# Modulation chunks of a two-layer block chain, summed over partitions by transposes and reductions in place of products with a pick matrix

## The chip, the cores and the metric

The kernel runs on one core of a Trainium2 chip. The metric is the device time of one launch in microseconds; the median of three runs of the kernel before is 2060.99 us (2060.79 to 2061.44). TensorE (PE) multiplies into PSUM, VectorE (DVE) and ScalarE (ACT) work beside it, and the loads go through the queue of SyncE (SP).

## What is computed

Two blocks of two layers each, on 256 tokens of width 1024. In the first block every layer has a modulation: a vector c (and in layer 0 a second one, c_ctx, for the context) goes through silu and a 1024 x 6144 matrix, and the six pieces of the result shift, scale and gate what the mixer and the feed-forward network (FFN) do.

```python
for i in range(DEPTH):
    mod = jax.nn.silu(c) @ w_ada[i] + b_ada[i]
    mod_c = jax.nn.silu(c_ctx) @ w_ada[i] + b_ada[i]
    sh1, sc1, g1, sh2, sc2, g2 = jnp.split(mod[:, None, :], 6, axis=-1)
    h = _modulate(_rms_norm(x, norm_mix[i]), sh1, sc1)
    ...
    x = x + g1 * y
    x = x + g2 * _swiglu(_modulate(_rms_norm(x, norm_ffn[i]), sh2, sc2), ffn_w_in[i], ffn_w_out[i])
```

Layer 0 mixes with a gated convolution (three 1024 x 1024 projections, then one out), layer 1 with attention. The second block (FFNs, two other mixers) has no modulation and is not touched.

## The kernel before

**Products and weights.** Each large product is made of three: high x high, low x high and high x low, where a float32 is split into a rounded high part and the rest (lines L243, L244, L245). Weights come in units of 512 KB through `WeightStream`: five raw buffers are loaded in a fixed order by SP, each unit is cast to whi on ACT (L106) and subtracted to wlo on DVE (L107) in two halves, with four buffers of whi and wlo. A raw buffer is loaded again when what reads it is done, so a unit that is used late holds back all loads behind it.

**Modulation chunks.** The modulation vector has 12 chunks of 512 columns in each layer. Some are made at the start by other functions. The other 20 are made by `ada_slow`, one (layer, j) at a time, of two vectors (12 chunks: layer 0, and layer 1 up to j = 3) or one (8 chunks). DVE multiplies the raw units with the values of the vector that lie in the partitions: per vector a TENSOR_SCALAR (L476) and seven multiply-adds (L478) of 128x512 into ada_acc. What is left is a sum over the 128 partitions. For it ada_acc is split into ada_hi (ACT, L251) and ada_lo (DVE, L252). A stage later PE multiplies each with `pick`, a matrix of ones and zeros in which one column picks the row of the vector (L489, L490; 2x512 in one PSUM bank), and ACT copies the two rows out (L492). Another stage later `ada_columns` turns the rows into columns by four small transposes (L441), and DVE adds the bias (L444) into mod.

**When they run.** `ada_slow` is a generator. The table ADA_AT starts a chunk at each of these points: the four groups of the convolution's input, groups 0 and 2 of its output for the first 256 tokens (chunks (0,8) and (0,9)), the ten groups of the FFN's hidden part and four of its output part. `ada_at` moves every pending generator on by one stage at each point; `ada_flush` ends them before the modulation of the FFN and of layer 1 needs them. The accumulators have two buffers for each vector (pool `ada`), so a chunk needs the buffer of the chunk two before it.

**What sets the order.** Each engine works through its instructions in a fixed order, which the framework's list scheduler makes from the program's order, the dependencies and its own estimates. So a change of one stage moves instructions of all engines around it. In conv_out (the convolution's output) the products of 256 columns go first for X (256 tokens, v = 0, four groups of 48 matmuls), then for C, the context; after a group DVE adds it to X (L546) and to a sum of squares (L558), and the row statistics (L361, Newton steps L265 to L269, L374, L376) precede the modulation of the FFN's input.

## Time and profile before

| what | us |
|---|---|
| median of three runs (2060.79 to 2061.44) | 2060.99 |
| the profiled execution | 2061.66 |
| its span in the trace | 2059.9 |
| PE busy | 2022.4 |
| DVE busy | 1522.6 |
| ACT busy | 1062.4 |

The profiled execution is 1.8 us longer than its span, the part of a launch that lies outside the trace. Times of places are us from the start of the span. A matmul's recorded length includes the time in the pipeline, so what one costs in a row is the distance to the next one's start.

### The profile page before, as it was taken

How to read it: one execution, taken by the hardware profiler on the slowest of the kernel's cores; microseconds unless marked ns; L12 is line 12 of the kernel's file. 1: busy time of each engine (PE TensorE's matmuls, PEld its weight loads, DVE VectorE, ACT ScalarE, POOL GpSimd, SP SyncE). 2: the span in 40 equal slices, each digit the busy share in tenths (PEclk: the TensorE clock that was granted, in tenths of full speed). 3: DMA queues.
4: the chain of work that ended last, by engine and by line, in shares of the span. 5: the costliest groups of instructions: out<-in, count | busy, mean ns of one | idle time of the engine just before them, and what ended most of it. 6: DMA issues, size and time to landing. Idle time of an engine off the chain costs nothing. (4 is left out here: it accounts for less than half of the span.)

```text
span 2059.9 us, 32409 instructions
## 1 busy us (share of the span) xinstructions
PE 2022.4 (98%) x12430; PEld 1776.4 (86%) x12430; DVE 1522.6 (74%) x2796; ACT 1062.4 (52%) x1763; POOL 4.1 (0%) x24
## 2 busy tenths in 40 slices
PE   7999999999999999999999999999999999999999
PEld 3888887888899999888888889998888888989888
DVE  6979998766377778766677667787767776887774
ACT  4534533323355566555455546555545554675552
POOL 0000000000000000000000000000000000000000
PEclk9999999999999999999999999999999999999999
DMA  7746566656254324466566564556656656425554
GB/s 249 230 144 195 174 206 197 219 189 200 89 165 148 98 88 137 138 186 188 180 190 186 178 189 137 151 171 189 189 176 192 185 183 190 138 83 166 186 180 133
DMA packets 327434, 350.93 MB, mean 170 GB/s; under 512 B 12592, under 2 KB 301488, under 8 KB 327280
## 3 DMA queue, kind: packets, MB, share of 16 engines
q1 hardware_dynamic: 327280, 348.88, 54.8%
q8 instruction: 97, 1.59, 0.3%
q14 instruction: 57, 0.47, 0.1%
HBM read 347.78 MB, written 1.05 MB: 169 GB/s over the span
## 5 line engine op out<-in xcount | busy, mean ns | idle before, releaser
L106 ACT CAST whi<-wraw 128x512 fp32r<-128x512 f32 (+1 forms) x803 | 617.0, 791 | 713.0 <-issue 245.4
L107 DVE TENSOR_TENSOR wlo<-wraw,whi 128x512 fp32r<-128x512 f32 (+1 forms) x803 | 709.5, 900 | 343.5 <-ACT whi L106 340.5
L306 PE MATMUL pg<-x,whi 128*128 128x512 f32 x1408 | 387.9, 397 | 0.5 <-DVE x L255 0.3
L306 PEld LDWEIGHTS pg<-x,whi 128*128 128x128 f32 x1408 | 241.0, 188 | 33.9 <-DVE x L255 2.8
L306 PE MATMUL po<-s,whi 128*128 128x512 f32 x880 | 243.0, 394 | 0.0
L308 PEld LDWEIGHTS pg<-x,wlo 128*128 128x128 f32 x1408 | 215.1, 188 | 31.8
L308 PE MATMUL pg<-x,wlo 128*128 128x256 f32 x1408 | 223.3, 280 | 0.0
L243 PE MATMUL pm<-xh,whi 128*128 128x512 f32 (+1 forms) x576 | 217.2, 381 | 2.8 <-ACT xh L251 2.8
L244 PE MATMUL pm<-xl,whi 128*128 128x512 f32 (+1 forms) x576 | 218.4, 380 | 0.0
L245 PE MATMUL pm<-xh,wlo 128*128 128x512 f32 (+1 forms) x576 | 217.9, 379 | 0.0
L478 DVE SCALAR_TENSOR_TENSOR ada_acc<-wraw,sil,ada_acc 128x512 f32<-128x512 f32 x224 | 159.6, 751 | 24.0 <-DMA wraw<-in_w_ada 22.6
L306 PEld LDWEIGHTS po<-s,whi 128*128 128x128 f32 x880 | 148.7, 189 | 18.0
L308 PEld LDWEIGHTS po<-s,wlo 128*128 128x128 f32 x880 | 137.5, 188 | 20.5
L308 PE MATMUL po<-s,wlo 128*128 128x256 f32 x880 | 142.5, 280 | 0.0
L243 PEld LDWEIGHTS pm<-xh,whi 128*128 128x128 f32 x576 | 109.1, 190 | 25.7 <-ACT xh L251 4.1
L244 PEld LDWEIGHTS pm<-xl,whi 128*128 128x128 f32 x576 | 109.5, 190 | 20.6 <-DVE xl L252 0.2
L245 PEld LDWEIGHTS pm<-xh,wlo 128*128 128x128 f32 x576 | 109.2, 190 | 20.5
L245 PE MATMUL pm<-sh,wlo 128*128 128x256 f32 (+1 forms) x384 | 119.3, 311 | 0.7 <-DVE wlo L107 0.7
L243 PE MATMUL pm<-sh,whi 128*128 128x256 f32 (+1 forms) x384 | 119.2, 311 | 0.0
L244 PE MATMUL pm<-sl,whi 128*128 128x256 f32 (+1 forms) x384 | 118.9, 310 | 0.0
L245 PE MATMUL pm<-whi,xl 128*128 128x256 f32 x352 | 99.7, 283 | 0.0
L306 PE MATMUL pg<-xh,whi 128*128 128x512 f32 x352 | 96.1, 394 | 0.0
(435 smaller groups left out, 3467.4 us busy)
## 6 DMA issues: line engine op xcount, KB each, us to landing
wraw<-in_ffn_w_in SPq DMA_DIRECT2D x264, 512.0 KB, 3.6
wraw<-in_ffn_w_out SPq DMA_DIRECT2D x128, 512.0 KB, 3.5
wraw<-in_w_ada SPq DMA_DIRECT2D x96, 512.0 KB, 4.5
wraw<-in_a_w_in SPq DMA_DIRECT2D x28, 512.0 KB, 3.8
wraw<-in_conv_w_in SPq DMA_DIRECT2D x24, 512.0 KB, 4.7
wraw<-in_attn_w_qkv SPq DMA_DIRECT2D x24, 512.0 KB, 4.0
wraw<-in_conv_w_out SPq DMA_DIRECT2D x16, 512.0 KB, 4.3
wraw<-in_ffn_w_out SPq DMA_DIRECT2D x28, 256.0 KB, 2.7
```

The lines of the kernel that those rows point to most:

```text
L106: self.nc.scalar.copy(hi[:, cs], raw[:, cs])
L107: self.nc.vector.tensor_tensor(lo[:, cs], raw[:, cs], hi[:, cs].bitcast(F32), ALU.subtract)
L243: mm(ps, ah, bh, start=first, stop=False)
L244: mm(ps, ah, bl, start=False, stop=False)
L245: mm(ps, al, bh, start=False, stop=last)
L306: self.nc.tensor.matmul(pss[c], hi[:, kk, cs], x2[:, done + kk], start=done + kk == 0, stop=False)
L308: self.nc.tensor.matmul(pss[c][:, 0, :], lo[:, kk, cs], x2[:, done + kk, 0, :], start=False, stop=done + kk == nblocks - 1)
L478: nc.vector.scalar_tensor_tensor(accs[v], w[:, kk, :], c, accs[v], ALU.mult, ALU.add)
```

## The change

Per chunk and vector the split into ada_hi and ada_lo is gone. At the chunk's next point PE transposes the four 128x128 blocks of ada_acc in fp32 into a PSUM bank, and DVE adds up each row of 128 by a TENSOR_REDUCE into a small tile ada_sum; one more addition puts the bias on, into mod. The products with pick, the row copy on ACT and the small transposes of these chunks are gone, and so is pick. The chunk is done one point earlier, while ada_acc is read by PE at that point and no longer only by ACT and DVE right after the last multiply-add.

```diff
--- before.py
+++ after.py
@@ -59,7 +59,7 @@
 NPACK = _pack_layout()
 CCOLS = {
     "ident": (0, 128), "upper": (128, 256), "tri_st": (256, 384),
-    "qk_both": (384, 640), "qk_low": (512, 640), "inv_freq": (640, 656), "pick": (656, 660),
+    "qk_both": (384, 640), "qk_low": (512, 640), "inv_freq": (640, 656)
 }
 NCONST = 660
 
@@ -397,8 +397,6 @@
     def ada_start(self):
         nc = self.nc
         sil = self.sil = self.cp.tile([P, 16], F32, name="sil")
-        self.pick = self.cp.tile([P, 4], F32R, name="pick")
-        nc.scalar.copy(self.pick, self.k("pick"))
         self.ada_pending = []
         nc.scalar.activation(sil, self.pk[:, 0:16], AF.Silu)
         self.c4 = self.cp.tile([P, KB, 4], F32R, name="c4")
@@ -434,13 +432,17 @@
         nc.vector.tensor_tensor(m, cv[:, :, :, 0], cv[:, :, :, 1], ALU.add)
         nc.vector.tensor_tensor(m, m, bias, ALU.add)
 
+    def mod_chunk(self, layer, j, vecs):
+
+        bias = self.p(f"b_ada{layer}")[:, 4 * j : 4 * j + 4, None].to_broadcast([P, 4, vecs])
+        return self.mod[:, layer, 4 * j : 4 * j + 4, 0:vecs], bias
+
     def ada_columns(self, layer, j, row):
 
         pt = self.aux_bank()
         for b in range(4):
             self.nc.tensor.transpose(pt[:, 2 * b : 2 * b + 2], row[0:2, b * P : (b + 1) * P], self.ident[0:2, 0:2])
-        bias = self.p(f"b_ada{layer}")[:, 4 * j : 4 * j + 4, None].to_broadcast([P, 4, 2])
-        m = self.mod[:, layer, 4 * j : 4 * j + 4, :]
+        m, bias = self.mod_chunk(layer, j, 2)
         self.nc.vector.tensor_tensor(m, pt[:, :8].rearrange("p (b v) -> p b v", b=4), bias, ALU.add)
 
     def ada_direct(self, layer, j):
@@ -477,21 +479,15 @@
                     else:
                         nc.vector.scalar_tensor_tensor(accs[v], w[:, kk, :], c, accs[v], ALU.mult, ALU.add)
             done += nk
-        parts = []
+        yield
+        col = self.small(8, "ada_sum")
         for v in range(vecs):
-            hi = self.adap.tile([P, 512], F32R, name="ada_hi", tag="hi")
-            lo = self.adap.tile([P, 512], F32R, name="ada_lo", tag="lo")
-            self.split(hi, lo, accs[v])
-            parts.append((hi, lo))
-        yield
-        ps = self.aux_bank()
-        for v, (hi, lo) in enumerate(parts):
-            nc.tensor.matmul(ps[0:2, :], self.pick[:, 2 * v : 2 * v + 2], hi, start=v == 0, stop=False)
-            nc.tensor.matmul(ps[0:2, :], self.pick[:, 2 * v : 2 * v + 2], lo, start=False, stop=v == vecs - 1)
-        row = self.tmp()
-        nc.scalar.copy(row[0:2, :], ps[0:2, :])
-        yield
-        self.ada_columns(layer, j, row)
+            pt = self.aux_bank()
+            for b in range(4):
+                nc.tensor.transpose(pt[:, b * P : (b + 1) * P], accs[v][:, b * P : (b + 1) * P], self.ident)
+            nc.vector.tensor_reduce(col[:, 4 * v : 4 * v + 4], pt.rearrange("p (b k) -> p b k", b=4), AX.X, ALU.add)
+        m, bias = self.mod_chunk(layer, j, vecs)
+        nc.vector.tensor_tensor(m, col[:, : 4 * vecs].rearrange("p (v b) -> p b v", b=4), bias, ALU.add)
 
     def ada_at(self, *at):
         self.ada_pending = [g for g in self.ada_pending if next(g, WAIT) is None]
```

How this stands in the engines' orders, at three places. In the changed file the lines are a little moved: TENSOR_SCALAR of a chunk is L478, the multiply-add L480, the transposes L487, the reduction L488, the last addition L490; the addition to X is L542 and the sum of squares L554.

PE in the FFN, in one of the hidden groups of layer 0, with a chunk of two vectors. Before:

```order
L245 MATMUL pm<-xh,wlo 128x512
L441 MATMUL pa<-kc,t 128x2 x4
L489 MATMUL pa<-ada_hi,pick 2x512
L490 MATMUL pa<-ada_lo,pick 2x512
L489 MATMUL pa<-ada_hi,pick 2x512
L490 MATMUL pa<-ada_lo,pick 2x512
L243 MATMUL pm<-xh,whi 128x512
```

After:

```order
L244 MATMUL pm<-xl,whi 128x512
L245 MATMUL pm<-xh,wlo 128x512
L487 MATMUL pa<-kc,ada_acc 128x128 x8
L243 MATMUL pm<-xh,whi 128x512
L244 MATMUL pm<-xl,whi 128x512
```

Four small transposes of one chunk and four products of the next have become eight transposes of the next.

DVE from the last conv group into conv_out. Before, where the last multiply-adds of chunk (0,7) run into the first of (0,8) and then the gate of the convolution (z, L849):

```order
L478 SCALAR_TENSOR_TENSOR ada_acc<-wraw,sil,ada_acc 128x512 x6
L107 TENSOR_TENSOR wlo<-wraw,whi 128x512 x2
L478 SCALAR_TENSOR_TENSOR ada_acc<-wraw,sil,ada_acc 128x512 x2
L476 TENSOR_SCALAR ada_acc<-wraw,sil 128x512 x2
L478 SCALAR_TENSOR_TENSOR ada_acc<-wraw,sil,ada_acc 128x512 x3
L107 TENSOR_TENSOR wlo<-wraw,whi 128x512 x2
L478 SCALAR_TENSOR_TENSOR ada_acc<-wraw,sil,ada_acc 128x512 x2
L849 TENSOR_TENSOR z_587<-pm,t 128x2x256
```

After, at the end of the same conv group (z is L845, its filter L848 and L849, its gate L851); the reductions are those of chunk (0,6), the TENSOR_SCALARs the first of (0,8), and L542 adds group 0 of conv_out to X:

```order
L849 SCALAR_TENSOR_TENSOR t<-z_586,pk,t 128x512
L488 TENSOR_REDUCE ada_sum<-pa 128x4
L851 TENSOR_TENSOR t<-pm,t 128x512
L488 TENSOR_REDUCE ada_sum<-pa 128x4
L478 TENSOR_SCALAR ada_acc<-wraw,sil 128x512
L252 TENSOR_TENSOR sl<-t,sh 128x512
L490 TENSOR_TENSOR mod<-ada_sum,pk 128x8
L478 TENSOR_SCALAR ada_acc<-wraw,sil 128x512
L480 SCALAR_TENSOR_TENSOR ada_acc<-wraw,sil,ada_acc 128x512 x2
```

The start of (0,8) has moved from ahead of the last conv group's end to behind the reductions of (0,6) that follow it.

PE after that, at the end of group 1 of conv_out (ada_acc here is that of (0,8)):

```order
L243 MATMUL pm<-sh,whi 128x256
L244 MATMUL pm<-sl,whi 128x256
L245 MATMUL pm<-sh,wlo 128x256
L487 MATMUL pa<-kc,ada_acc 128x128 x8
L245 MATMUL pm<-sh,wlo 128x256
L243 MATMUL pm<-sh,whi 128x256
```

The transposes of (0,8), and with them all of its multiply-adds, now stand between the products of groups 1 and 2.

## Rows read from the trace of the kernel before

**Rows 1.** The page's first row: PE's busy time, its share of the span and its instructions; the same for PE's weight loads (PEld), DVE, ACT and POOL.

```profile
PE 2022.4 (98%) x12430; PEld 1776.4 (86%) x12430; DVE 1522.6 (74%) x2796; ACT 1062.4 (52%) x1763; POOL 4.1 (0%) x24
```

**Rows 2.** Windows: one stretch in a row, us from the start of the span. Columns: the stretch, its length, busy us (and instructions) of PE, PEld, DVE, ACT and POOL, the granted clock of TensorE, the share of DMA, GB/s. First four rows of conv_out, one behind the row statistics of C, two rows of the FFN of layer 0, and one of the attention of layer 1, in which transposes of 128x128 stand.

```profile
185.00:195.00 10.00, 10.00 (x81) 8.92 (x80) 9.96 (x20) 4.18 (x9) 0.00 (x0) 1.00 0.53 160
195.00:205.00 10.00, 10.00 (x82) 9.51 (x81) 8.04 (x17) 4.92 (x10) 0.00 (x0) 1.00 0.70 204
205.00:215.00 10.00, 8.81 (x64) 7.55 (x64) 9.39 (x18) 6.28 (x13) 0.00 (x0) 1.00 0.52 166
215.00:230.00 15.00, 15.00 (x126) 14.79 (x126) 13.77 (x39) 8.59 (x18) 0.00 (x0) 1.00 0.69 209
253.00:256.00 3.00, 3.00 (x18) 3.00 (x17) 3.00 (x6) 3.00 (x7) 0.00 (x0) 0.56 0.02 5
300.00:350.00 50.00, 50.00 (x226) 40.32 (x225) 42.59 (x71) 16.70 (x30) 0.00 (x0) 1.00 0.60 189
500.00:560.00 60.00, 60.00 (x270) 49.04 (x269) 25.75 (x43) 19.14 (x34) 0.00 (x0) 1.00 0.38 119
690.00:705.00 15.00, 15.00 (x126) 14.33 (x125) 9.19 (x18) 7.04 (x15) 0.00 (x0) 1.00 0.25 71
```

**Rows 3.** Timeline of PE in conv_out: start, length in us, engine, line, operation, out<-in, and in brackets the idle time ahead of it with what ended it. The first row is the first instruction behind conv group 3, the last the statistics matmuls of X.

```profile
180.03 0.41 PE L441 MATMUL pa<-kc,t 2*128 2x2 f32 x4
...
206.67 0.39 PE L245 MATMUL pm<-sh,wlo 128*128 128x256 f32 x1 [0.73 <-DVE wlo L107]
...
209.31 0.39 PE L489 MATMUL pa<-ada_hi,pick 128*2 128x512 f32 x1 [0.46 <-ACT ada_hi L251]
...
215.61 0.38 PE L361 MATMUL pa<-mean,acc 128*128 128x1 f32 x2
```

**Rows 4.** The waits from 60 to 620 us: engine, line and tile that waits, what it waits for, us in total, times, longest.

```profile
PE pm L243 <- ACT xh L251: 1.9, 1, 1.9
...
PE pa L376 <- DVE t L374: 1.1, 1, 1.1
```

**Rows 5.** Timeline of PE at four places: a chunk of two vectors (the last product ahead of it and the first behind), a chunk of one vector, four fp32 transposes L1076, and eight fp32 transposes L1029, each with the products around it.

```profile
332.35 0.39 PE L245 MATMUL pm<-xh,wlo 128*128 128x512 f32 x1
...
333.92 0.39 PE L243 MATMUL pm<-xh,whi 128*128 128x512 f32 x1
...
448.33 0.39 PE L245 MATMUL pm<-sh,wlo 128*128 128x512 f32 x1
...
449.45 0.39 PE L243 MATMUL pm<-xh,whi 128*128 128x512 f32 x1
...
663.54 0.28 PE L245 MATMUL pm<-whi,xl 128*128 128x256 f32 x1
...
664.22 0.28 PE L244 MATMUL pm<-wlo,xh 128*128 128x256 f32 x1
...
698.20 0.28 PE L244 MATMUL pa<-ptl,vh 128*128 128x256 f32 x1
698.32 0.28 PE L245 MATMUL pa<-pth,vl 128*128 128x256 f32 x1
...
699.43 0.28 PE L244 MATMUL pm<-wlo,xh 128*128 128x256 f32 x1
```

**Rows 6.** Groups of instructions by line and form: out<-in, partitions x elements, count | busy us in all, mean ns of one | idle time ahead and what ended it. PE, then DVE, then ACT.

```profile
L1076 PE MATMUL pa<-kc,t 128*128 128x128 f32 x128 | 17.1, 273 | 0.6 <-DVE rc_g L269 0.6
...
L252 DVE TENSOR_TENSOR ada_lo<-ada_acc,ada_hi 128x512 fp32r<-128x512 f32 x32 | 21.5, 689 | 0.6 <-PE pa L490 0.4 <-ACT ada_hi L251 0.2
...
L1274 DVE TENSOR_REDUCE mst<-pa 128x2 f32<-128x512 f32 x8 | 5.5, 682 | 0.0
...
L251 ACT CAST ada_hi<-ada_acc 128x512 fp32r<-128x512 f32 x32 | 19.1, 618 | 3.0 <-DVE ada_acc L478 2.5 <-PE pa L489 0.4
...
L492 ACT COPY t<-pa 2x512 f32<-2x512 f32 x20 | 11.4, 571 | 0.0
```

**Rows 7.** Timeline of DVE beside conv group 3 and in conv_out. L476 and L478 with ada_acc are the multiplications of a chunk (those that begin at 162.39 are chunk (0,8), those at 206.54 the end of chunk (0,9)).

```profile
162.39 0.89 DVE L476 TENSOR_SCALAR ada_acc<-wraw,sil 128x512 f32<-128x512 f32 x2 [0.62 <-DMA wraw<-in_w_ada]
163.18 1.41 DVE L478 SCALAR_TENSOR_TENSOR ada_acc<-wraw,sil,ada_acc 128x512 f32<-128x512 f32 x2
...
178.10 0.76 DVE L478 SCALAR_TENSOR_TENSOR ada_acc<-wraw,sil,ada_acc 128x512 f32<-128x512 f32 x1
...
206.54 2.73 DVE L478 SCALAR_TENSOR_TENSOR ada_acc<-wraw,sil,ada_acc 128x512 f32<-128x512 f32 x4
209.18 0.69 DVE L107 TENSOR_TENSOR wlo<-wraw,whi 128x512 fp32r<-128x512 f32 x1
209.78 1.29 DVE L252 TENSOR_TENSOR ada_lo<-ada_acc,ada_hi 128x512 fp32r<-128x512 f32 x2
```

**Rows 8.** DMA from 185 to 215 us, GB/s moved in 40 equal slices of 0.75 us, and from the page the loads of conv_w_out: count, KB each, median us from issue to landing.

```profile
GB/s 0 0 27 167 352 330 344 175 14 0 78 313 315 53 231 322 86 78 335 294 93 265 255 122 255 299 86 38 0 0 61 337 300 4 227 375 93 169 348 234
...
wraw<-in_conv_w_out SPq DMA_DIRECT2D x16, 512.0 KB, 4.3
```

**Rows 9.** Timeline of PE at the row statistics of C.

```profile
247.90 0.28 PE L245 MATMUL pm<-xh,wlo 128*128 128x256 f32 x1
249.25 0.67 PE L376 MATMUL pa<-t,ones 128*128 128x256 f32 x2 [1.08 <-DVE t L374]
251.86 0.93 PE L243 MATMUL pm<-xh,whi 128*128 128x256 f32 x4 [1.94 <-ACT xh L251]
```

## The prediction

> **What bounds the kernel now.** I read the page's first row, then the windows by stage, the waits of the stretch in which the changed code runs, and the timelines of PE and DVE there. PE is busy 98% of the span, DVE 74% and ACT 52% [rows 1]. The changed code runs from about 60 to 592 us, and the windows separate three kinds of stretch [rows 2]. In the FFN (300 to 560 us) PE is busy in every us, while DVE has 25.75 of 60 to 42.59 of 50 us: PE work taken away there is time gained. In conv_out (185 to 215 us) DVE is busy 9.96, 8.04 and 9.39 of each 10 us, so that stage is carried by two engines at once. Behind it PE falls to 8.81 of 10 us, with two waits: 0.73 us for wlo, from DVE, and 0.46 for ada_hi, from ACT [rows 3]. The waits of 60 to 620 us hold little else for PE's matmuls: 1.9 us for xh and 1.1 for t, each once [rows 4].

> **TensorE's products, columns and transposes.** Prices are distances of starts, since the busy time of a pipelined matmul overlaps the next. Over a chunk of two vectors PE goes from 332.35 (last matmul ahead) to 333.92 (next one), 1.57 us, of which 0.23 is the ordinary distance: four small column transposes and four 512-wide products cost 1.34 us. Over a chunk of one vector it is 448.33 to 449.45, 1.12 less 0.23, so 0.89 us [rows 5]. The same fp32 128x128 transposes stand in the trace elsewhere: eight of L1029 between 698.32 and 699.43, 1.11 us less two distances of 0.12, so 0.87; four of L1076 between 663.54 and 664.22, 0.68 less 0.24, so 0.44 [rows 5]. A chunk therefore gains 0.47 (two vectors, 12 chunks) or 0.45 (one, 8 chunks), in all 5.6 + 3.6 = **9.2 us of PE**. Six of the two-vector chunks lie in the conv block, worth 2.8 us; the other 14 lie in the FFN, 6 x 0.47 + 8 x 0.45 = **6.4 us**. There the accumulators are held for one group longer, but a chunk's multiplications take some 10 us of DVE (below), and DVE is idle for 7.4 of 50 us in the busiest FFN window, in which PE never stops [rows 2]; I see nothing there that takes the 6.4 away.

> A recorded transpose lasts 273 ns [rows 6], far more than 0.109. [...] If each held PE for its recorded time, the sum would come out on the other side; that is rival D.

> **DVE and ACT.** Per vector a subtraction ada_lo (689 ns) becomes a reduction from PSUM. The nearest row, L1274 from PSUM with the same input, takes 682 ns; per chunk the small addition stays. DVE's load stays the same. ACT loses 32 casts of 618 ns and 20 copies of 571 ns, some 31 us [rows 6], and the copy of pick at the start. ACT bounds none of the stretches of [rows 2], so all this is costed at nothing; the cover is its idle half.

> **The order on DVE in conv_out.** This is the new cost. Before, an accumulator was free once DVE and ACT had split it. Now it is held until PE has transposed it, one point of the program later, and the chunk after next needs the same buffer. For chunk (0,8) that means the transposes of (0,6), which stand at the end of conv group 3. Before, (0,8) was multiplied on DVE from 162.39, and its last step began at 178.10, beside conv group 3, which ends on PE at 180.03 [rows 3, 7]. The changed order puts its first TENSOR_SCALAR behind a reduction of (0,6). So 2 x 0.40 + 14 x 0.66 = 10.0 us of DVE work move behind 180 us, into the stretch that had 2.6 of 30 us of DVE idle.

> I replayed the changed order from there with distances of starts: a 256-wide matmul 0.12 (a conv_out group of 48: 5.8), the multiply-add 0.66, the halves of wlo and a reduction 0.60 [rows 5, 7]. PE ends conv group 3 at 179.5 (0.07 + 0.47 earlier) and has the transposes out by 180.3. DVE then has, in the changed order, four reductions (2.4), two TENSOR_SCALAR (0.8), ten multiply-adds (6.6), the last two steps of the convolution (1.2) and small additions (1.3), 12.3 us from 180.2 on; the second wlo of group 1 is ready at 193.1. PE needs it at 190.8: it stands **2.3 us**. Four more multiply-adds end at 196.35; PE stands 0.6 us for them at the transposes of (0,8), and group 2 ends at 202.3. DVE now has chunk (0,9) ahead of group 3's first wlo, ready 208.35: PE has eaten what lies ahead by 202.75 and stands **5.6 us**, then 1.2 for the next wlo and 0.6 for the last multiply-adds of (0,9). It reaches the statistics matmuls L361 of X at 219.7, with seven matmuls fewer behind it than before, so at equal work at 220.55 against 215.61 [rows 3]: **+4.9 us**. All of this chunk work's PE gain is inside that number.

> It hangs also on loads: the first unit of group 2 takes a raw buffer that (0,8) frees at 189.85. With the 4.3 us from issue to landing [rows 8] and a cast it is ready at 194.8, not 193.1, which makes the shift +6.2. I take **+5.5**, near the middle; bounds are below 0 (the wlo of group 3 not late) and the +11 of rival C. [...]

> One more place: in the row statistics of C, multiply-adds of (0,10) stand between the small steps on DVE, and PE waits behind them for t [rows 9]. Two of them become TENSOR_SCALAR (0.40 for 0.66): **-0.5** (0 to -0.5).

> **The sum.** Profiled execution 2061.66 - 6.4 + 5.5 + 0.5 - 0.5 = 2060.8, a change of -0.9. The profiled execution is 0.67 above the median of the three runs, 2060.99; the median should become **2060.1 us**. Against some 0.2% (4.1 us, about what a measurement of this kernel can tell from no change) that is no difference. Large parts cancel: the FFN's gain and the loss in conv_out.

> **Rivals.**
> - A, the forecast: DVE late in conv_out, 2060.1. For it: the order and a DVE without idle time. Its own range is 2056.5 to 2063.
> - B, no new stand. DVE would catch up: in conv_out it has 2.6 us idle, and PE's old waits (0.73 and 0.46) may vanish. Then the whole 9.2 us stays: 2060.99 - 9.2 = 2051.8, with the waits and C's steps about 2050.5. Against it: 10.0 us of work in 2.6 us of idle time.
> - C, slower: the loads fall behind too. Five units (four of (0,9), then group 3's first) queue up behind (0,8)'s last buffer, freed at 196.35. I took them at 1.6 us each, which the fastest slices of [rows 8] allow (512 KB at 330 GB/s); at the mean of conv_out, 160 to 209 GB/s [rows 2], it is 2.6 us. [...] It decides once a load takes over 2 us there.
> - D: each transpose holds PE for its recorded 273 ns. 128 x (0.273 - 0.109) = +21.0, less 9.2, gives 2072.8. The distances in [rows 5] speak against it.

> **How the numbers follow.** A 0.62 (of it 0.03 faster, 0.57 within, 0.02 slower), B 0.21, C 0.13, D 0.04. Faster by over 0.2%: 0.24; within: 0.57; slower: 0.19. The range from 2051.5 to 2065.5 leaves out D, the lower part of B and the upper of C.

> **What would show it.** Right: between 190 and 216 us PE has a wait of about 2 and one of about 5 us for wlo L107, DVE is without idle time from 180 to 215, and L361 of X starts some 4 to 5 us later than 215.61; from 300 to 592 us the same work is 6.4 us shorter. B is right if L361 comes earlier than 215.61; C if PE's long wait is for whi, and ACT's for a load; D if eight L487 take over 2 us from the matmul ahead to the one behind. Wrong altogether if PE waits in the FFN, for a transpose's ada_acc or a wlo: then the longer held accumulators cost there as well.

## The result and the profile after

| kernel | median, us | lowest to highest | runs |
|---|---|---|---|
| before | 2061.47 | 2058.99 to 2063.57 | 20 |
| changed | 2065.12 | 2059.61 to 2068.62 | 20 |

The ratio is 1.0018, with a 95% interval of 1.0012 to 1.0025: the changed kernel is slower, by 3.7 us in the medians. The forecast was 0.9 us faster. The profiled execution of the changed kernel took 2062.32 us with a span of 2060.5, at the low side of its runs. One execution of all the kernels below is left out of the numbers: 2185.75 us at a mean granted clock of 0.849, of the changed kernel with three accumulators, its tiles moved by 64 bytes.

The page's first row, to be read against [rows 1]: 16 matmul records fewer and 5.6 us less of PE's busy time, 28 us less of ACT's, DVE as before. Nothing in it says where time was lost.

```profile
PE 2016.8 (98%) x12414; PEld 1782.9 (87%) x12414; DVE 1523.4 (74%) x2796; ACT 1034.4 (50%) x1710; POOL 4.1 (0%) x24
```

The windows of the changed kernel, columns as in [rows 2]: conv_out in four stretches, then two pieces of it by themselves, the place behind the row statistics of C, an FFN stretch, and the attention stretch with transposes.

```profile
185.00:195.00 10.00, 7.45 (x63) 7.24 (x62) 10.00 (x19) 2.25 (x5) 0.00 (x0) 1.00 0.35 109
195.00:205.00 10.00, 9.77 (x70) 9.57 (x68) 8.82 (x18) 2.10 (x5) 0.00 (x0) 0.83 0.79 260
205.00:215.00 10.00, 4.69 (x22) 4.49 (x23) 10.00 (x18) 3.72 (x7) 0.00 (x0) 0.72 0.48 141
215.00:230.00 15.00, 15.00 (x124) 15.00 (x123) 13.85 (x37) 7.14 (x15) 0.00 (x0) 0.96 0.78 232
196.00:199.00 3.00, 3.00 (x16) 3.00 (x16) 3.00 (x6) 0.00 (x0) 0.00 (x0) 0.50 0.84 272
211.00:216.00 5.00, 4.95 (x23) 4.96 (x24) 5.00 (x8) 2.28 (x4) 0.00 (x0) 0.50 0.72 214
...
258.00:261.00 3.00, 2.06 (x17) 2.06 (x18) 3.00 (x7) 3.00 (x8) 0.00 (x0) 1.00 0.10 35
...
300.00:350.00 50.00, 50.00 (x230) 41.60 (x229) 42.51 (x70) 15.73 (x28) 0.00 (x0) 1.00 0.63 190
...
690.00:705.00 15.00, 15.00 (x125) 14.32 (x125) 9.20 (x18) 7.03 (x15) 0.00 (x0) 1.00 0.25 71
```

In conv_out PE falls from 10.00 and 8.81 to 7.45 and 4.69 of 10 us, while DVE is busy for 10.00, 8.82 and 10.00: PE stands (sits idle and waits) for DVE, as forecast. Two pieces behind PE's stands have a granted clock of 0.50 (196 to 199 and 211 to 216 us). In the FFN PE is still never idle.

PE in conv_out, columns as in [rows 3]: the transposes L487, every wait, and the statistics matmuls of X.

```profile
180.39 1.03 PE L487 MATMUL pa<-kc,ada_acc 128*128 128x128 f32 x8
...
187.02 1.03 PE L487 MATMUL pa<-kc,ada_acc 128*128 128x128 f32 x8
194.43 0.38 PE L245 MATMUL pm<-sh,wlo 128*128 128x256 f32 x1 [2.55 <-DVE wlo L107]
197.84 1.67 PE L487 MATMUL pa<-kc,ada_acc 128*128 128x128 f32 x8
206.35 0.38 PE L243 MATMUL pm<-sh,whi 128*128 128x256 f32 x1 [1.58 <-ACT whi L106]
211.05 0.58 PE L245 MATMUL pm<-sh,wlo 128*128 128x256 f32 x1 [3.95 <-DVE wlo L107]
...
223.15 0.28 PE L361 MATMUL pa<-mean,acc 128*128 128x1 f32 x2
```

The first stand is the forecast 2.3 us. The forecast 5.6 us for wlo came as 1.58 for whi and 3.95 for wlo; its three smaller stands (0.6, 1.2, 0.6) do not show as idle time. L361 comes 7.54 us later than in [rows 3]. The stage began 0.36 us later (180.39 against 180.03), so it is 7.2 us longer. By then PE has issued 222 products of 256 columns, 229 before: the seven fewer that the prediction counted. At 0.12 us each the stage is 8.0 us longer at equal work.

DVE there, columns as in [rows 7]:

```profile
183.20 0.47 DVE L478 TENSOR_SCALAR ada_acc<-wraw,sil 128x512 f32<-128x512 f32 x1
...
190.38 3.40 DVE L480 SCALAR_TENSOR_TENSOR ada_acc<-wraw,sil,ada_acc 128x512 f32<-128x512 f32 x5
193.69 1.28 DVE L107 TENSOR_TENSOR wlo<-wraw,whi 128x512 fp32r<-128x512 f32 x2
...
203.38 0.48 DVE L542 SCALAR_TENSOR_TENSOR X<-pm,mod,X 128x256 f32<-128x256 f32 x1 [0.62 <-PE pm L245]
...
204.81 0.48 DVE L542 SCALAR_TENSOR_TENSOR X<-pm,mod,X 128x256 f32<-128x256 f32 x1 [0.56 <-PE pm L245]
...
210.31 1.29 DVE L107 TENSOR_TENSOR wlo<-wraw,whi 128x512 fp32r<-128x512 f32 x2
```

Chunk (0,8) begins at 183.20, where it began at 162.39 [rows 7]; its multiply-adds at 190.38 stand ahead of the wlo at 193.69 for which PE waits from 191.88. At 203.38 and 204.81 DVE waits for PE in turn.

The waits from 60 to 620 us, columns as in [rows 4]:

```profile
PE pm L245 <- DVE wlo L107: 6.5, 2, 4.0
...
PE pm L243 <- ACT xh L251: 2.0, 1, 2.0
...
PE pm L243 <- ACT whi L106: 1.6, 1, 1.6
...
PE pa L376 <- DVE t L374: 0.2, 1, 0.2
```

Two long stands for wlo (one of 0.73 us before [rows 3]) and one for whi are new; that for t, 1.1 us before [rows 4], is nearly gone. The same list has ACT's waits for the loads of conv_w_out, before and then changed:

```profile
ACT whi L106 <- DMA wraw<-in_conv_w_out: 6.1, 6, 2.6
...
ACT whi L106 <- DMA wraw<-in_conv_w_out: 16.9, 10, 4.5
```

So the loads do come later, a sign that the prediction gave for rival C; the one stand of PE that follows from it is the 1.58 us for whi. The row statistics of C, columns as in [rows 9]:

```profile
256.30 0.65 PE L376 MATMUL pa<-t,ones 128*128 128x256 f32 x2
258.94 0.74 PE L243 MATMUL pm<-xh,whi 128*128 128x256 f32 x4 [1.99 <-ACT xh L251]
```

One stand of 1.99 us is left where there were two, and the clock of 258 to 261 us stays at 1.00, where the like place had 0.56 [rows 2]. From L361 of C to the first chunk of the FFN it is 45.24 us (247.26 to 292.50), 1.8 less than before.

Most of these 1.8 us are not the change. The changed kernel run again (e4 below) has the same single stand of 1.99 us, and the clock falls behind it; the kernel before with its tiles moved by 64 bytes (also below) has both stands, and it does not:

```profile
261.00:264.00 3.00, 3.00 (x17) 3.00 (x17) 3.00 (x6) 2.66 (x6) 0.00 (x0) 0.54 0.42 126
...
253.00:256.00 3.00, 3.00 (x25) 2.90 (x26) 3.00 (x6) 3.00 (x8) 0.00 (x0) 1.00 0.27 90
```

With one fall this stretch takes 47.07 us before and 46.56 in e4; with none it takes 45.71 in the moved kernel before and 45.24 in the changed one. At a like clock the gain is 0.5 us.

A chunk of two vectors in the FFN, columns as in [rows 5]:

```profile
337.60 0.39 PE L245 MATMUL pm<-xh,wlo 128*128 128x512 f32 x1
337.83 1.04 PE L487 MATMUL pa<-kc,ada_acc 128*128 128x128 f32 x8
338.62 0.48 PE L243 MATMUL pm<-xh,whi 128*128 128x512 f32 x1
338.93 0.39 PE L244 MATMUL pm<-xl,whi 128*128 128x512 f32 x1
```

From 337.60 to 338.93 are 1.33 us. Less two distances of 0.227 the chunk costs 0.88; 0.87 was forecast, 1.34 was the cost before. The groups by form, columns as in [rows 6], give the new instructions: a transpose is recorded with 279 ns, a reduction takes 680 ns, as forecast from L1274.

```profile
L488 DVE TENSOR_REDUCE ada_sum<-pa 128x4 f32<-128x512 f32 x32 | 21.3, 680 | 0.0
L487 PE MATMUL pa<-kc,ada_acc 128*128 128x128 f32 x128 | 17.9, 279 | 0.0
```

From the first chunk of the FFN to the L361 behind it the time goes from 307.09 to 301.07 us, so -6.0, with -6.4 forecast. At that point (593.57 us, 593.85 before) the changed kernel is 0.28 us ahead. **All that the change edits is over by then, and the sum stands as forecast.** The loss lies behind it, in code that nobody touched: from the first product with pth (676.53 in the changed kernel, 676.54 before; pth is a tile of the attention of layer 1) to the end of the span it is 1384.0 us against 1383.4. That is little of the 3.7 us of the medians; the executions below show the rest.

The windows of 100 us of the two kernels say what differs there. PE is never idle in any of them, so the count of matmuls is its pace. First before: an FFN whose products take xh and xl, then two whose products take the tile x2 (the trace calls it x).

```profile
860.00:960.00 100.00, 100.00 (x572) 87.38 (x571) 65.53 (x64) 56.47 (x64) 0.00 (x0) 1.00 0.63 189
1400.00:1500.00 100.00, 100.00 (x570) 87.16 (x570) 74.43 (x72) 55.46 (x62) 0.00 (x0) 1.00 0.60 184
1600.00:1700.00 100.00, 100.00 (x573) 87.30 (x572) 73.09 (x71) 54.45 (x62) 0.00 (x0) 1.00 0.59 183
```

The same windows of the changed kernel:

```profile
860.00:960.00 100.00, 100.00 (x571) 87.34 (x571) 64.54 (x63) 56.29 (x65) 0.00 (x0) 1.00 0.62 191
1400.00:1500.00 100.00, 100.00 (x568) 87.17 (x567) 73.62 (x72) 55.35 (x62) 0.00 (x0) 1.00 0.60 185
1600.00:1700.00 100.00, 100.00 (x569) 87.18 (x568) 71.89 (x70) 54.46 (x62) 0.00 (x0) 1.00 0.58 179
```

At a granted clock of 1.00 the products with x2 run 0.4 to 0.7% slower, those with xh as before. By the program these products are the same in both kernels; what differs for them is where their operands lie. Bytes per partition, from the built kernels:

```
                             whi (first of 4)   xh       x2       x2 - whi
before                       80224              112992   204768   124544
changed                      80256              113024   204768   124512
```

The change drops the tile pick (one slot of 32 bytes) and adds ada_sum (two slots), so all tiles allocated behind them move up by 32 bytes. x2 is allocated from the other end and stays. xh moves together with the weights, x2 doesn't.

### The profile page after: what moved, and what is told of

It reads as the page before. It is cut to its first block, busy times and chain, and to the rows that moved or that the text cites. A ratio compares the mean times of both kernels' runs of the same rounds, so it can differ in the third digit from the quotient of the medians.

```text
span 2060.5 us, 32318 instructions
## 1 busy us (share of the span) xinstructions
PE 2016.8 (98%) x12414; PEld 1782.9 (87%) x12414; DVE 1523.4 (74%) x2796; ACT 1034.4 (50%) x1710; POOL 4.1 (0%) x24
## 5 line engine op out<-in xcount | busy, mean ns | idle before, releaser
L107 DVE TENSOR_TENSOR wlo<-wraw,whi 128x512 fp32r<-128x512 f32 (+1 forms) x803 | 709.0, 898 | 376.2 <-ACT whi L106 374.7
L480 DVE SCALAR_TENSOR_TENSOR ada_acc<-wraw,sil,ada_acc 128x512 f32<-128x512 f32 x224 | 157.6, 745 | 1.3
```

Of the source, the lines that this page charges most:

```text
L107: self.nc.vector.tensor_tensor(lo[:, cs], raw[:, cs], hi[:, cs].bitcast(F32), ALU.subtract)
L480: nc.vector.scalar_tensor_tensor(accs[v], w[:, kk, :], c, accs[v], ALU.mult, ALU.add)
```

## The experiments

The theory after the first reading: the accumulators, held longer, make DVE late in conv_out; the FFN gains; what is left over comes from the place of the tiles. Rivals: transposes that cost more than forecast, loads that fall behind, and a clock that falls in PE's stands.

**A third accumulator.** With a third buffer DVE need not wait for the transposes of (0,6).

```diff
-        accs = [self.adap.tile([P, 512], F32, name="ada_acc", tag=f"acc{v}") for v in range(vecs)]
+        accs = [self.adap.tile([P, 512], F32, name="ada_acc", tag=f"acc{v}", bufs=3) for v in range(vecs)]
```

> The changed kernel with three buffers in place of two for each of the accumulators ada_acc, and nothing else. Theory H (held accumulators): the loss sits in conv_out alone, where chunk (0,8) must wait for the transposes of (0,6), so DVE is late, PE stands for wlo and the clock falls behind each stand. A third buffer lets (0,8) run beside the last conv group again: no stand over 1 us of PE between 185 and 222 us, granted clock 1.00 there, and the whole 9.2 us of PE of the prediction come through: 2051 to 2054 us, some 12 us below the changed kernel. Theory P (the transposes themselves, by their length or by not counting for the clock): the third buffer changes none of them, 2062 us or more, and the clock falls remain.

Measured: 2057.76 us (2053.80 to 2060.41, 11 runs), ratio to before 0.9984 [0.9975, 0.9993]. In conv_out it does what the theory says, with PE busy in 8.25, 10.00 and 8.98 of the three stretches of 10 us from 185 us and

```profile
214.96 0.28 PE L361 MATMUL pa<-mean,acc 128*128 128x1 f32 x2
```

8.2 us earlier than in the changed kernel. But the total gains 5.9 us only (against e4, the changed kernel run again on the same chip), and in the profiled execution the untouched part behind pth takes 1388.5 us. No theory that I had gave both numbers. The 1388.5 goes with the clock of that execution (mean 0.993; 0.994 in the changed kernel's): without what the clock took off, an estimate that the last section explains, the part takes 1379.1 us, and 1380.1 in the changed kernel.

**One half of the change at a time.** The old route was kept beside the new one: for the chunks of the conv block (layer 0, j below 10) in the first kernel, for all others in the second, with pick in both. What the branch holds is the lines of the kernel before.

```diff
+        if layer == 0 and j < 10:
...
+            return
```

> The old route (split, products with pick, row copy, small transposes) for the six chunks (0,4) to (0,9) of the conv block, the new one for the 14 chunks of the FFN. Theory H: conv_out as in the kernel before, the FFN shorter by the 6.0 to 6.4 us that the two traces show there: 2055 to 2056 us. Theory P: the transposes cost in the FFN too, no gain: 2060 to 2062.

> The reverse: the new route for the six chunks of the conv block, the old one for the 14 of the FFN. Theory H: the whole loss of conv_out and none of the gain, so 6 us above the changed kernel: 2070 to 2072 us, and a spread of the runs as wide as that of the changed kernel (9 us in 20 runs, against 4.6 before), since the spread would come from how long the clock stays low behind the stands. Theory P: 2064 to 2066, the loss shared between both stages.

> The changed kernel once more, for a second trace and more runs. Theory H with a varying clock: the same two stands of 2 to 4 us in conv_out, but the stretch of half clock behind them of another length; the median again 2064 to 2066. If the wide spread came from the loads instead, the stands themselves would differ by several us and the clock would not.

Measured: new route in the FFN alone 2046.97 (2044.75 to 2047.95, 5 runs), 0.9933 [0.9919, 0.9946]; in the conv block alone 2057.28 (2053.28 to 2060.37, 11), 0.9982 [0.9973, 0.9991]; the changed kernel beside them (e4) 2063.64 (2061.56 to 2067.37, 11), 1.0017 [1.0008, 1.0025]. Both halves are some 8 to 15 us faster than was expected, and together they would make the change a gain of 16 us. With pick and ada_sum both there, these kernels have their tiles 64 bytes higher than before. Behind pth they take 1373.7 and 1374.0 us.

**Only the place.** Place +32 means that the tiles allocated from the left, the weights among them, start 32 bytes per partition higher than in the kernel before, while x2 stays. Nothing but a tile is made longer: 32 bytes more for c4 (8 floats; 16 floats for 64), which is allocated ahead of the weight buffers. The moved kernels issue the same instructions in the same order as the one they were made from; only addresses differ.

```diff
-        self.c4 = self.cp.tile([P, KB, 4], F32R, name="c4")
+        c4 = self.cp.tile([P, KB * 4 + 8], F32R, name="c4")
+        self.c4 = c4[:, : KB * 4].rearrange("p (k f) -> p k f", f=4)
```

> The kernel before, with one constant tile 32 bytes per partition longer, so that everything allocated behind it on the left side of SBUF (weights whi and wlo, activations xh, the stores of the later stages) starts 32 bytes higher, as in the changed kernel, while the tile x2 of the second block, allocated from the right, stays. No instruction and no order changes. Theory L (layout): the changed kernel is slower because dropping pick and adding ada_sum moved the left side by 32 bytes, and products of x2 with whi and wlo keep another pace then: the part behind 676 us (first product with pth) goes from 1383 to 1384 to 1387 us and the median from 2060.3 to 2061 to 2064. Theory H (held accumulators explain it all): no change, 2060.3.

> The same with 64 bytes, the place that the left side has in the two kernels with both routes (both keep pick and add ada_sum). Theory L: the part behind 676 us takes 1374 us as it did there, the median 2050 to 2052, with nothing of the change in the kernel. Theory H: 2060.3, and the two mixed kernels would remain unexplained.

> The changed kernel with its left side at the place of the kernel before (ada_sum is taken from the pool of the accumulators, and one constant tile is 32 bytes longer); the same instructions in the same order. Theory L: what is left is the change itself as the prediction added it up, conv_out's loss against the FFN's gain: 2059 to 2062, no difference from the kernel before by more than 2 us; behind 676 us 1383. Theory H: as the changed kernel, 2064.

> The changed kernel with its left side 64 bytes above that of the kernel before, as in the two mixed kernels. Theory L: behind 676 us 1374, the median 2051 to 2054, and within 2 us of the kernel before at the same place. Theory H: 2064.

(For e7 ada_sum comes from another pool that lies elsewhere, so that the 32 bytes of c4 put all other tiles back where they were before.)

| kernel | place against before | median, us (n) | ratio to before, 95% | behind pth, us |
|---|---|---|---|---|
| before moved | +32 | 2065.26 (11) | 1.0023 [1.0014, 1.0031] | 1385.2 |
| before moved | +64 | 2052.04 (5) | 0.9958 [0.9944, 0.9971] | 1374.0 |
| changed, moved back | 0 | 2060.53 (11) | 0.9999 [0.9990, 1.0008] | 1382.8 |
| changed, moved on | +64 | 2053.59 (5) | 0.9967 [0.9955, 0.9980] | 1373.0 |

Here is the cause: the kernel before, moved as the change moves it, loses 4.5 us by itself, and the change at an unmoved place costs nothing that can be measured. The windows of the kernel before at +64, same stretches as above:

```profile
860.00:960.00 100.00, 100.00 (x572) 87.34 (x571) 64.75 (x63) 56.36 (x64) 0.00 (x0) 1.00 0.62 190
1400.00:1500.00 100.00, 100.00 (x580) 87.74 (x579) 75.22 (x73) 56.17 (x64) 0.00 (x0) 1.00 0.61 189
1600.00:1700.00 100.00, 100.00 (x578) 87.63 (x577) 74.35 (x76) 55.05 (x64) 0.00 (x0) 1.00 0.60 188
```

580 and 578 matmuls where before had 570 and 573, and 572 again with xh. The kernel before at +32 and the changed kernel moved back to 0, each from 1400 to 1500 us:

```profile
1400.00:1500.00 100.00, 100.00 (x567) 87.10 (x566) 74.84 (x72) 54.83 (x62) 0.00 (x0) 1.00 0.59 185
...
1400.00:1500.00 100.00, 100.00 (x572) 87.24 (x572) 74.25 (x72) 56.17 (x63) 0.00 (x0) 1.00 0.59 185
```

In starts of PE (means behind 860 us, clock 1.00), a product of x with wlo follows another after 115.7 ns at +64, 117.4 at 0 and 118.6 (changed kernel) or 119.0 (before moved) at +32; products of xh with whi after 233.6 at all three. ACT and DVE write the weight buffers meanwhile, but that is not the difference: for the 84 or 85 such products that start while neither of them works, the means are 115.9, 117.8 and 119.4 or 120.4 ns.

**The distance or the address?** x2 was moved down by 64 bytes and the weights left where they are.

```diff
-        return net.xp2.tile([P, KB, 2, T], F32R, name="x2", tag="x2")
+        return net.xp2.tile([P, KB * 2 * T + 16], F32R, name="x2", tag="x2")[:, : KB * 2 * T].rearrange("p (k s t) -> p k s t", k=KB, s=2)
```

> The kernel before with x2 alone 64 bytes lower (its tile is 64 bytes longer, at the right end); weights and all else stay. The distance from x2 to the weights is then that of the kernel before moved by 64, at other absolute addresses. Theory R (the pace depends on the distance of the two operands): behind 676 us 1374, the median 2051 to 2053. Theory A (it depends on where the weights themselves start): 1383 and 2060.7 as before.

Measured: 2050.10 (2048.85 to 2052.78, 5), 0.9946 [0.9933, 0.9958], 1374.2 behind pth and 579 matmuls from 1400 to 1500 us. As with the weights moved up: the distance from whi to x2 is 124480 in both, so it is the distance from x2 to the tiles on the left that counts, not one tile's own address.

**Third accumulator and place together.** Place +64, place +96, and place +64 with every transpose issued twice (the second writes the same values again).

```diff
-            for b in range(4):
+            for b in (0, 1, 2, 3, 0, 1, 2, 3):
```

> The changed kernel with three accumulator buffers and the left side 64 bytes above that of the kernel before. If the two causes add up (conv_out's stands, 7 us, and the layout, 13 us against 32 bytes): 2057.8 less 11 to 13, so 2044.5 to 2047, below every kernel so far, and some 7 us below the changed kernel at the same place (2053.6). If conv_out's gain was an accident of one place: 2052 to 2054.

> The same kernel 32 bytes further. It asks whether the pace has a period of 64 bytes (then as at 32 bytes: 2057 to 2060) or changes with each step (0: 0 us, 32: +4.5, 64: -8.7 so far, so nothing can be said but that it lies between 2040 and 2060).

> The kernel with three buffers and 64 bytes, every transpose of ada_acc issued twice into the same place (the sum is read from the second). The price of the prediction, 0.44 us for four transposes: 12 x 0.87 + 8 x 0.44 = 14 us more than the kernel without the second, 2058.5 to 2061; rival D, the recorded 273 ns each: 35 us more, 2080.

Measured: at +64 from 2041.4 to 2044.1 (3 runs), 0.9908 [0.9893, 0.9923]; at +96 2048.59 (2046.72 to 2050.79, 5), 0.9937 [0.9923, 0.9950], with 1379.1 us behind pth, so between the places 64 and 0; with transposes twice 2055.42 (2050.81 to 2057.92, 6), 0.9969 [0.9958, 0.9980]. 128 more transposes cost some 12 to 13 us, 0.10 us each. The trace agrees: in the FFN 16 in a row cost 1.76 us (334.67 to 336.88, less two distances) where the 8 of the changed kernel cost 0.88, so 0.11 each. Rival D, 273 ns each, would be 35 us.

**At an unmoved place again.** The third accumulator, and the new route in the FFN alone, with all tiles where they were before; and the changed kernel (at its own place, +32) with idle products of ones, whose result nobody reads, at PE's stands for wlo, to hold the clock. Of the last one's edit only the new lines are shown.

```diff
...
+                        if v == 0 and (g, u) in ((1, 1), (3, 0)):
+                            fill = net.aux_bank()
+                            for _ in range(3 if u else 6):
+                                nc.tensor.matmul(fill, net.ones, net.kc[:, 128:640], start=True, stop=True)
```

> The changed kernel with three accumulator buffers, its left side at the place of the kernel before, so that only the change of route is left. If the prediction's two large terms were right and only the layout was missed: conv_out's loss (7 to 8 us by the traces) goes, the 9.2 us of PE stay, 2051 to 2053 us. If the layout hides another loss of the change: 2056 or more.

> Old route in the conv block, new one in the FFN, left side at the place of the kernel before. The FFN term alone: 2060.7 less 6.0 to 6.4, 2054 to 2055 us. If the gain of the FFN is given back later: 2060.

> The changed kernel with idle products (fp32, 128x512, of two constants, result unused) ahead of the second unit of conv_out's group 1 (three) and ahead of group 3 (six), where PE stands for wlo. DVE's work is untouched, so the stands for DVE remain, filled. If the clock that falls behind the stands is a large part of conv_out's loss (4 us at half pace by the trace): L361 of X comes 2 to 4 us earlier than 223, granted clock 1.00 from 185 to 222 us, 2061 to 2062.5 us. [...]

Measured: 2054.07 (2048.65 to 2054.41, 5), 0.9964 [0.9952, 0.9976]; 2055.05 (2050.31 to 2057.01, 6), 0.9969 [0.9956, 0.9981]; 2066.27 (2064.10 to 2071.35, 5), 1.0033 [1.0021, 1.0046]. The first came out 1 to 3 us above what was expected, with conv_out at 33.9 us; the second as expected. The windows of the third:

```profile
195.00:205.00 10.00, 9.93 (x66) 8.11 (x65) 9.78 (x21) 1.26 (x4) 0.00 (x0) 1.00 0.70 232
205.00:215.00 10.00, 7.83 (x37) 6.19 (x36) 8.54 (x14) 3.70 (x7) 0.00 (x0) 0.83 0.55 162
```

The clock is 1.00 and 0.83 where the changed kernel had 0.83 and 0.72, and yet conv_out takes 43.9 us (179.11 to 223.00) against 42.8. Of the difference 0.7 us are six products that stand ahead of L361 here and behind it in the changed kernel. DVE's two waits for PE, 0.62 and 0.56, are gone, but DVE waits for ACT in their place:

```profile
206.46 0.43 DVE L554 TENSOR_TENSOR acc<-acc,t 128x256 f32<-128x256 f32 x1 [1.67 <-ACT t L548]
```

ACT's square of X (L548) ran behind a cast of whi that had waited 2.12 us for a load. So holding the clock made the stage no shorter, but the clock was held only in part, and another wait took what DVE got back: what the falls cost by themselves is not shown.

**All of it at the changed kernel's own place.** Third accumulator, tiles at +32, x2 32 bytes lower: the distance is again 124480.

> The changed kernel with three accumulator buffers, its left side where the change puts it (32 bytes up), and x2 32 bytes lower. The distance of x2 to the weights is then that of the kernel moved by 64. Theory R (distance): 2042 to 2045, as the kernel with three buffers moved by 64 (2043.2), behind 676 us 1374. If the start of the weights themselves mattered: 2057.8, as with three buffers alone.

Measured: 2041.62 (2039.17 to 2045.77, 4), 0.9901 [0.9884, 0.9918], 20.9 us below the kernel before on the same chip; with the same buffers at +64 (2041.4 to 2044.1) it is the fastest of all. Its pace in the stretch of x2:

```profile
1400.00:1500.00 100.00, 100.00 (x578) 87.62 (x577) 73.55 (x75) 55.31 (x63) 0.00 (x0) 1.00 0.60 185
```

The places side by side, medians in us (for the changed kernel at +32 those of e4 and of the 20 runs; for three accumulators at +64 the middle of three runs). They come from several chips, on which the kernel before takes 2060.15 to 2062.50:

| | 0 | +32 | +64 | +96 |
|---|---|---|---|---|
| before | 2060.8 | 2065.3 | 2052.0 | |
| changed | 2060.5 | 2063.6, 2065.1 | 2053.6 | |
| changed, three accumulators | 2054.1 | 2057.8 | 2042.3 | 2048.6 |

## Why the prediction was wrong

The step that failed is the one that ends "so all this is costed at nothing": dropping the copy and the tile pick, and (not even named) adding the tile ada_sum. As work they do cost nothing. As bytes they moved every weight buffer by 32 against x2, and that costs 4.5 us (ratio 1.0023 for the kernel before, moved). Put back in place the change gives 0.9999 [0.9990, 1.0008], -0.2 us, where the prediction had -0.9. No rival had this mechanism, so it is luck that 2065.12 lies in the stated range. Rival C's shift of +11 in place of +5.5 would come to the same number (2060.99 - 6.4 + 11 - 0.5 = 2065.1), but not in this way: no run shows the +11, the stage is 8.0 us longer at equal work, and the extra 5.5 us in conv_out would have stayed in the unmoved kernel, and didn't. A part of C is there: ACT waits for the loads, and PE stands 1.58 us for whi at 206.35.

Point by point:

- **FFN, -6.4.** Right in mechanism, a little too large. The prices held (0.88 for 0.87 with two vectors; 0.44 for 0.44 with one, 450.98 to 451.87 less two distances), and the trace gives -6.0. Every profiled execution with the new route there has 301.0 to 301.2 us (with every transpose twice 309.8), every one with the old 307.1 to 307.5. Timed at an unmoved place it is -5.1 in the medians (2060.15 to 2055.05), and at +64 the same -5.1 (2052.04 to 2046.97, two chips); the ratio's interval, -9.1 to -3.9 us, holds all these. PE had no wait there for an accumulator.
- **conv_out, +5.5 (4.9 to 6.2).** The mechanism was right: the order on DVE, the two late stretches and their places. The size was too small: counted from the start of the stage the forecast is 6.0 (5.5 and the 0.5 us that its replay lets PE come early), the trace gives 8.0 at equal work. The long stands are near the forecast (2.55 for 2.3; 1.58 and 3.95 for 5.6), though the 1.58 was for whi. What the replay left out is that PE works at a granted clock of 0.50 behind them (196 to 199 and 211 to 216 us), and that DVE then waits for PE twice, 0.62 and 0.56. That these make up the rest was read from the rows; the kernel with the idle products has neither wait, but lost the time elsewhere, so it is not shown. That the order is the cause was tried: a third accumulator takes the stage from 42.6 to 33.9 us at the unmoved place.
- **Clock, the +0.5 of the sum, and C, -0.5.** No run shows the +0.5. What the traces show is a granted clock of 0.50 behind the long stand of 3.95 us (211 to 216 us) and behind the first one of 2.55 us (196 to 199 us), and that the stage got no shorter where the idle products held the clock at 1.00 and 0.83 from 195 to 215 us. What the falls cost is open, as said above. C is -0.5 at a like clock, as forecast; the -1.8 of the profiled pair has a fall of the clock in it that one execution had and the other not. From the start of the stage to the first chunk of the FFN, where all work is made up again, it is 106.73 us before and 113.45 in e4, which has the same fall there: +6.7, where 6.0 + 0.5 - 0.5 was forecast. That this sum is near is in part luck: 2.0 too little in conv_out, and some 1.3 less behind it, the seven late products included. Timed, the conv block with its C is +5.2 (2057.28 against 2052.04 at +64, two chips).
- **D.** The records of the fp32 transposes are 279 ns long, but 128 more of them cost 0.10 us each; the measurement decides.
- **Place.** The prediction had no term for it. Between the places tried the kernel before goes from 2052.04 (+64) to 2065.26 us (+32), and a product of x with wlo from 115.7 to 119.0 ns.

**What stays open.** Why a distance of 124480 bytes is good and 124512 bad is not shown; places were tried in steps of 32 bytes only, and whether it is the distance to whi, to wlo or to another tile can't be told apart, since these move together. That it is x2's distance is shown; what in the chip makes it so is not. How far the four buffers of a weight tile differ among themselves wasn't tried.

## What to carry to other kernels

An edit that adds or drops a tile can move all tiles behind it, as here by 32 bytes, which cost 4.5 us; before the result is put down to the edit, run the kernel before with the same move, and the changed kernel with the move undone. When a step hands a buffer on one point later in the program, look for who needs that buffer next: here some 9 us of the stage hung on two buffers against three (42.6 against 33.9). A difference in code that nobody touched, at the same granted clock and with an engine that is never idle, is a reason to try other places for its operands.
